# A third buffer for raw weights, and layer norms centred on ACT and scaled on GpSimd, in a hybrid decoder kernel on Trainium2

## The chip, the cores and the metric

The kernel runs on one core of a Trainium2 chip. Its engines run side by side, each through its own instructions in order: TensorE (PE in the profile; PEld its weight loads) multiplies matrices, VectorE (DVE) and ScalarE (ACT) do elementwise work, GpSimd (POOL) elementwise work of a slower kind, and SyncE (SP) issues the transfers. The metric is the device time of one execution in microseconds (us).

## The reference

Two layers over 512 tokens of width 1024, all in fp32. The four attention groups A to D are of 256 columns each; their inside is left out here.

```python
for l in range(DEPTH):                                  # DEPTH = 2
    h = x @ w_in[l]
    ...                                                 # out_a, out_b, out_c, out_d from parts of h
    mix = jnp.concatenate([out_a, out_b, out_c, out_d], axis=-1)
    y = _group_rmsnorm(mix, mix_g[l]) @ w_o[l]
    x = _layernorm(ALPHA * x + y, ln1_g[l], ln1_b[l])
    f = (jax.nn.silu(x @ w_gate[l]) * (x @ w_up[l])) @ w_down[l]      # width 2816
    x = _layernorm(ALPHA * x + f, ln2_g[l], ln2_b[l])

def _layernorm(x, g, b, eps=1e-5):
    mu = jnp.mean(x, axis=-1, keepdims=True)
    var = jnp.mean(jnp.square(x - mu), axis=-1, keepdims=True)
    return (x - mu) * lax.rsqrt(var + eps) * g + b
```

## The kernel before

The residual stream `x_res` stays on chip as four token tiles of 128 tokens by 1024, and is handled in halves of 512 columns. For matmuls x is also kept transposed (`xT`). To keep fp32 accuracy every operand is split into a high part (a rounded copy, on ACT or POOL) and a low part (operand minus high part, line 442, on DVE or POOL), and each product is made in three passes: high by high, high by low, low by high.

**Weights.** A `Chunk` is 128 x 1024 of weights: it is loaded into a raw buffer (`w_raw`, a ring of two), then `copy` makes the high part and `split_lo` the low part, into rings of their own (`w_hi`, `w_lo`; for the first two feature tiles `qk`, a ring that the attention has left by then). A loader takes the chunks in order as raw buffers come free, and a splitter follows.

**The order of the work** comes from a list scheduler in the program: every instruction is an `Op` with an engine, a cost and a priority, and the scheduler lays them one by one on the five in-order queues by their modelled earliest start and, within a slack, by priority. `sched.best` picks between engines the one that would end first. So an edit that changes one cost or engine moves others too.

**The stage around the change.** The last piece of a layer's attention is the out-projection of groups A and B, `out_proj(GA, GB)`. TensorE makes, per token tile and half, a product for A and one for B (six matmuls `ps<-w_hi/w_lo/v,mix` each, line 464), first for token tiles 0 and 1, then for 2 and 3. DVE adds each to `x_res` (line 1743); the add of B also sums the row for the norm. Then `layernorm` works tile by tile: ACT squares (L803), small DVE operations on columns of `lnst` (L810 to L840, L477 to L481, all 128 x 1), and two passes over each half on DVE:

```python
DVE.scalar_tensor_tensor(out=centred[c], in0=centred[c], scalar=st[:, 5:6], in1=gb[c], op0=ALU.add, op1=ALU.mult)   # L853: (x - mu) * gain
DVE.scalar_tensor_tensor(out=x[:, t, csl], in0=centred[c], scalar=st[:, 9:10], in1=bb[c], op0=ALU.mult, op1=ALU.add)  # L858: * rsqrt(var) + bias
```

The normed half is transposed by TensorE (L751, four 128 x 128), copied by ACT (the high part of xT, L453) and subtracted on DVE (its low part, L442); for ln1 another ACT copy (`keep`, L1801, a lower priority) stores the transposed tile for later. A tile counts as transposed for the next stage once that copy is laid on its queue. Next come the first two feature tiles, `up(0, 1)`: gate and up weights of 128 columns each, on half of the tokens at a time (24 matmuls `ps<-xT,qk` of 256 columns per weight and half). The first half of the tokens needs token tiles 0 and 1 only, and so can run while tiles 2 and 3 are still being normed.

ln1 stands at this place in both layers. ln2 of layer 0 follows the feed-forward (add on line 2003, gain in `mixf`, bias in `vd`), and the next layer's input projection uses `xT` behind it. ln2 of layer 1 ends the program; it is called with `hurry=True`. POOL also multiplies the residual by ALPHA after ln2 (L772).

Of the kernel before, what the change touches and what calls it, by code (L numbers as in the profile page):

```python
# [29 lines left out]
P = 128  # L30
S = 512
D = 1024
NT = S // P
# [13 lines left out]
GA, GB, GC, GD = range(4)  # L47
# [18 lines left out]
E_PE, E_ACT, E_DVE, E_POOL, E_SP = range(5)  # L66
# [22 lines left out]
def c_act(n, psum=True, extra=0):  # L89
    return (52.0 if psum else 94.0) + 0.832 * n + 93.0 * extra  # L90
# [14 lines left out]
def c_pool2(n):  # L105
    return 147.0 + 2.11 * n
# [13 lines left out]
class Sched:  # L120
# [232 lines left out]
def trunk(ctx: ExitStack, tc: tile.TileContext, d):  # L353
# [4 lines left out]
    spawn = sched.spawn  # L358
# [133 lines left out]
    class Chunk:  # L492


        def __init__(self, kt, n, parts, custom=None, rings=None, both=None, low=E_POOL, n_split=None, gate=None):
            self.kt, self.n, self.parts, self.custom = kt, n, parts, custom
            self.r_hi, self.r_lo = rings or (r_hi, r_lo)
            self.both, self.n_split, self.low, self.gate = both, n_split or n, low, gate
            self.raw = self.part = self.dep = self.loaded = None

        weight = 1

        def raw_room(self):
            return r_raw.ready()

        def view(self, tile_, n):
            return tile_[:, :self.kt * n].rearrange("p (k n) -> p k n", n=n)

        def load(self):
            self.raw = r_raw.take()  # L510
            e = NOW
            for k0, k1, c0, c1, src in self.parts:
                size = (k1 - k0) * (c1 - c0) * (2 if c1 - c0 < P else 1)
                e = yield from dma(self.view(self.raw.tile, self.n)[:, k0:k1, c0:c1], src, 1.46 * size / 1024, self.raw.dep)
            self.loaded = e
# [276 lines left out]
    def layernorm(t, vecs, st, dep, later, then, hurry=False):  # L792

        gb, bb, loaded, _ = vecs
        prio = LOW if hurry and t < NT - 1 else 0

        def square(c, dep):
            yield lambda: r_temp.ready()  # L800
            junk = r_temp.take()
            a = yield Op(E_ACT, c_act(512, False, 2), join(dep, junk.dep))
            ACT.activation(out=junk.tile, in_=x[:, t, c * 512:(c + 1) * 512], func=AF.Square, bias=st[:, 2:3], scale=1.0 / 32,  # L803
                           accum_out=st[:, 3 + c:4 + c])
            junk.give(a)
            squared[c] = a

        squared = {}
        e = yield Op(E_DVE, 130.0, dep)
        DVE.tensor_scalar(out=st[:, 2:3], in0=st[:, 0:1], scalar1=-1.0 / (32 * 512), scalar2=0.0, op0=ALU.mult, op1=ALU.add)  # L810
        spawn(square(0, e), 0, t - NT)
        second = yield later
        spawn(square(1, join(e, second)), 0, t - NT)
        e = yield Op(E_DVE, 130.0, second, prio)
        DVE.tensor_scalar(out=st[:, 5:6], in0=st[:, 1:2], scalar1=st[:, 0:1], scalar2=-1.0 / D, op0=ALU.add, op1=ALU.mult)
        centred = [x[:, t, :512], x[:, t, 512:]]
        held, early = [], {}
        if hurry and t == NT - 1:

            def centre(e):  # L820
                yield lambda: r_temp.ready(2)
                held.extend([r_temp.take(), r_temp.take()])
                for c in range(2):
                    g = yield Op(E_DVE, 663.0, join(e, loaded, held[c].dep))
                    DVE.scalar_tensor_tensor(out=held[c].tile, in0=centred[c], scalar=st[:, 5:6], in1=gb[c],
                                             op0=ALU.add, op1=ALU.mult)
                    centred[c] = held[c].tile
                early["done"] = g

            spawn(centre(e), 0, t - NT)  # L830
        b = yield Op(E_DVE, 130.0, second)
        DVE.tensor_scalar(out=st[:, 6:7], in0=st[:, 1:2], scalar1=st[:, 0:1], scalar2=1.0 / D, op0=ALU.subtract, op1=ALU.mult)
        a = yield lambda: squared.get(0)
        b = yield Op(E_DVE, 130.0, join(a, b))
        DVE.tensor_scalar(out=st[:, 7:8], in0=st[:, 6:7], scalar1=st[:, 6:7], scalar2=st[:, 3:4], op0=ALU.mult, op1=ALU.subtract)
        a = yield lambda: squared.get(1)

        def scale():
            r = yield Op(E_DVE, 130.0, join(a, b))
            DVE.tensor_scalar(out=st[:, 8:9], in0=st[:, 4:5], scalar1=st[:, 7:8], scalar2=1e-5, op0=ALU.subtract, op1=ALU.add)  # L840
            if hurry:
                squared["r"] = yield Op(E_POOL, 464.0, r)
                rsqrt(st[:, 9:10], st[:, 8:9])
            else:
                squared["r"] = yield from rsqrt_1(st[:, 9:10], st[:, 8:9], st[:, 10:13], r)

        spawn(scale(), 0, t - NT)
        if hurry and t == NT - 1:
            e = yield lambda: early.get("done")
        else:  # L850
            for c in range(2):
                e = yield Op(E_DVE, 663.0, join(a, e, loaded), prio)
                DVE.scalar_tensor_tensor(out=centred[c], in0=centred[c], scalar=st[:, 5:6], in1=gb[c], op0=ALU.add, op1=ALU.mult)  # L853
        r = yield lambda: squared.get("r")
        for c in range(2):
            csl = slice(c * 512, (c + 1) * 512)
            e = yield Op(E_DVE, 663.0, join(a, r, e), prio)
            DVE.scalar_tensor_tensor(out=x[:, t, csl], in0=centred[c], scalar=st[:, 9:10], in1=bb[c], op0=ALU.mult, op1=ALU.add)  # L858
            if c:
                x_dep[t] = e  # L860
            then(t, c, e)
        for h in held:
            h.give(e)


    def layer(l):
# [5 lines left out]
        at = {}  # L872
# [635 lines left out]
        class Uses:  # L1508


            def __init__(self, held, n):
                self.held, self.joint = held, Joint(n, held.give)
# [209 lines left out]
            return out  # L1722


        added = {(t, c): Joint(3) for t in range(NT) for c in range(2)}

        def out_proj(*groups, last=None):

            cs = {g: [Chunk(1, D, [(0, 1, 0, D, rows(d["w_o"][l], 2 * g + k, 1))],
                            both=r_v if len(groups) > 1 and g == groups[0] and k == 0 else None) for k in range(2)]  # L1730
                  for g in groups}
            chunks.extend(c for pair in cs.values() for c in pair)
            blocks = ((0, 1), (2, 3)) if len(groups) > 1 else ((0, 1, 2, 3),)
# [135 lines left out]
        def up(*js):  # L1869
            cs = {}  # L1870
            for j in js:
                for n in ("w_gate", "w_up"):
                    cs[n, j] = Chunk(KT, P, [(0, KT, 0, P, rows(d[n][l][:, j * P:(j + 1) * P], 0, KT))],
                                     rings=(r_qk, r_qk) if len(js) > 1 else None, low=E_DVE if len(js) > 1 else None,
                                     gate=(lambda: ("mix", GB) in at) if len(js) > 1 else None)
            chunks.extend(cs.values())
            toks = HALVES if len(js) > 1 else (ALL,)

            def unit():
                ps, ready = {}, {}  # L1880
# [250 lines left out]
        low = E_DVE  # L2131
# [140 lines left out]
```

## Time and profile before

| | |
|---|---|
| median of 3 runs | 1220.42 us (1219.75 to 1221.94) |
| the profiled execution | 1220.06 us, its span 1218.3 us |
| mean granted TensorE clock | 0.992 |
| instructions | 20162 |
| busy: PE, DVE, ACT, POOL | 97%, 73%, 56%, 20% of the span |
| ln1 of layer 0, about | 235 to 266 us |
| ln2 of layer 0, about | 592 to 617 us |
| ln1 of layer 1, about | 840 to 871 us |

A row of the timeline reads: start, duration, engine, line, operation, written tile <- read tiles, shape, how many instructions the row holds; in brackets the engine's idle time ahead of it and what ended that. A duration includes the tail of an instruction that already overlaps with the next on the same engine, so the distance of two starts is often shorter.

### The profile page before, as it was taken

Reading aid. Unit: us, or ns where it says so; the run is one execution under the profiler, and the core shown is the slowest. Engines: PE = TensorE matmul, PEld = TensorE weight load, DVE = VectorE, ACT = ScalarE, POOL = GpSimd, SP = SyncE. Lnnn points to the kernel's source line nnn. Section 1 sums busy time; section 2 is a strip of 40 time slices with the busy share of each in tenths; the row PEclk is TensorE's granted clock in tenths of the full one; section 3 lists DMA queues with packets and bytes.
Section 4 is the critical chain, followed back from the end, with each engine's and each line's share of the span. In section 5 each row is a group of like instructions: output and inputs, shape, how many; then the busy total and the mean of one; then the engine's idle time right before and its main releaser. Section 6 shows DMA issues by size and latency. Waiting matters only on the chain.

```text
span 1218.3 us, 20162 instructions
## 1 busy us (share of the span) xinstructions
PE 1180.2 (97%) x7589; PEld 1069.5 (88%) x7589; DVE 892.1 (73%) x1699; ACT 685.7 (56%) x1441; POOL 241.4 (20%) x243
## 2 busy tenths in 40 slices
PE   8999999989999999999999999999899999999996
PEld 7979878779999989998799797778899989899985
DVE  5669668799896649873655895788998947499626
ACT  4759869456564325553356797684665634256421
POOL 3552765300000000000034536543000000000001
PEclk9999999999999999999999999999999999999999
DMA  6312230423333133324233211203233341343341
GB/s 201 88 47 63 57 104 12 128 87 87 105 105 120 48 128 105 105 92 130 72 71 87 57 53 56 87 27 113 87 90 119 96 131 51 108 119 88 104 138 70
DMA packets 112162, 110.75 MB, mean 91 GB/s; under 512 B 9792, under 2 KB 94656, under 8 KB 112064
## 3 DMA queue, kind: packets, MB, share of 16 engines
q1 hardware_dynamic: 112064, 109.45, 29.9%
q8 instruction: 60, 0.98, 0.3%
q14 instruction: 38, 0.31, 0.1%
HBM read 107.34 MB, written 2.10 MB: 90 GB/s over the span
## 4 chain that ended last, share of the span: by engine, by line
PE 79%; DVE 9%; ACT 5%; issue 3%; POOL 2%; DMA 0%; POOLq 0%; SPq 0%; DVEq 0%; ACTq 0%
PE ps L464 76%; PE ps L1557 1%; DVE x_res L1743 1%; POOL w_lo L442 1%; PE ps L751 1%; DVE xT L442 1%; DVE qk L442 1%; ACT temp L1445 1%; DVE pt L442 1%; ACT pt L1363 1%; DVE x_res L858 1%; ACT xT L722 0%; DVE qk L444 0%; DVE temp L1306 0%; DVE augk L1092 0%
## 5 line engine op out<-in xcount | busy, mean ns | idle before, releaser
L464 PE MATMUL ps<-xT,w_hi 128*128 128x256 f32 (+1 forms) x1128 | 215.5, 318 | 0.0
L464 PEld LDWEIGHTS ps<-xT,w_hi 128*128 128x128 f32 x1128 | 162.4, 191 | 11.4
L464 PE MATMUL ps<-w_hi,qk 128*128 128x512 f32 (+1 forms) x560 | 171.5, 388 | 0.0
L464 PE MATMUL ps<-xT,w_lo 128*128 128x256 f32 (+1 forms) x888 | 166.0, 304 | 0.0
L722 ACT CAST w_hi<-w_raw 128x1024 fp32r<-128x1024 f32 (+2 forms) x91 | 92.8, 1021 | 108.1 <-PE ps L464 90.5
L442 POOL TENSOR_TENSOR w_lo<-w_raw,w_hi 128x1024 fp32r<-128x1024 f32 (+4 forms) x66 | 120.9, 1837 | 106.4 <-ACT w_hi L722 76.3
L442 DVE TENSOR_TENSOR w_lo<-w_raw,w_hi 128x1024 fp32r<-128x1024 f32 x47 | 57.6, 1225 | 111.6 <-ACT w_hi L722 111.5
L464 PEld LDWEIGHTS ps<-xT,w_lo 128*128 128x128 f32 x888 | 123.7, 191 | 7.3
L464 PEld LDWEIGHTS ps<-w_hi,qk 128*128 128x128 f32 x560 | 104.6, 189 | 20.9
L464 PE MATMUL ps<-w_hi,mix 128*128 128x512 f32 x352 | 110.1, 394 | 3.1 <-DVE xT L442 1.8
L464 PE MATMUL ps<-w_lo,qk 128*128 128x512 f32 (+1 forms) x280 | 108.2, 387 | 0.0
L1911 ACT COPY temp<-ps 128x256 f32<-128x256 f32 x120 | 44.7, 373 | 85.2 <-PE ps L464 84.7
L659 ACT CAST w_hi<-temp 128x512 fp32r<-128x512 f32 x78 | 48.3, 620 | 64.9 <-DVE temp L602 35.6
L772 POOL TENSOR_SCALAR x_res<-x_res 128x1024 f32<-128x1024 f32 x8 | 9.4, 1180 | 375.3 <-DVE lnst L840 357.2
L464 PEld LDWEIGHTS ps<-w_hi,mix 128*128 128x128 f32 x352 | 64.6, 188 | 16.4 <-issue 2.1
L442 DVE TENSOR_TENSOR w_hi<-temp,w_hi 128x512 fp32r<-128x512 f32 x78 | 53.2, 687 | 30.7 <-ACT w_hi L659 30.5
L467 POOL TENSOR_TENSOR lnst<-lnst,mhalf 128x1 f32<-128x1 f32 x4 | 3.9, 985 | 362.2 <-DVE lnst L840 362.2
L659 ACT CAST w_lo<-temp 128x512 fp32r<-128x512 f32 x82 | 50.8, 621 | 42.7 <-DVE temp L602 28.1
L464 PE MATMUL ps<-xT,qk 128*128 128x256 f32 x528 | 69.1, 291 | 2.0 <-DVE qk L442 2.0
L464 PE MATMUL ps<-w_lo,mix 128*128 128x512 f32 x176 | 69.0, 392 | 1.9 <-POOL w_lo L442 1.9
L464 PE MATMUL ps<-w_hi,xT 128*128 128x388 f32 (+1 forms) x256 | 69.1, 351 | 0.4 <-DVE qk L444 0.4
L464 PEld LDWEIGHTS ps<-xT,qk 128*128 128x128 f32 x528 | 66.8, 199 | 2.8 <-DVE qk L442 2.6
(234 smaller groups left out, 2692.5 us busy)
## 6 DMA issues: line engine op xcount, KB each, us to landing
w_raw<-in_w_down SPq DMA_DIRECT2D x44, 512.0 KB, 3.8
w_raw<-in_w_in SPq DMA_DIRECT2D x26, 512.0 KB, 3.7
w_raw<-in_w_gate SPq DMA_DIRECT2D x24, 512.0 KB, 3.7
w_raw<-in_w_up SPq DMA_DIRECT2D x24, 512.0 KB, 3.7
w_raw<-in_w_o SPq DMA_DIRECT2D x16, 512.0 KB, 3.7
vd<-in_w_up SPq DMA_DIRECT2D x10, 512.0 KB, 3.7
mixf<-in_w_up SPq DMA_DIRECT2D x10, 512.0 KB, 3.7
vd<-in_w_gate SPq DMA_DIRECT2D x10, 512.0 KB, 4.9
```

Of the source, the lines that this page charges most:

```text
L442: eng.tensor_tensor(out=lo, in0=src, in1=f(hi), op=ALU.subtract)
L464: PE.matmul(out, lhsT=lhsT, rhs=rhs, start=start, stop=stop, skip_group_check=True)
L659: ACT.copy(out=self.part[0], in_=src)
L722: ACT.copy(out=out, in_=in_ if psum is None else psum)
L751: PE.transpose(out=u.tile[:, k * P:(k + 1) * P], in_=x[:, t, kk * P:(kk + 1) * P], identity=ident)
L772: POOL.tensor_scalar(out=x[:, t], in0=x[:, t], scalar1=ALPHA, scalar2=0.0, op0=ALU.mult, op1=ALU.add)
L858: DVE.scalar_tensor_tensor(out=x[:, t, csl], in0=centred[c], scalar=st[:, 9:10], in1=bb[c], op0=ALU.mult, op1=ALU.add)
L1363: ACT.copy(out=dst[0], in_=src)
L1445: ACT.activation(out=p[:, s_], in_=ps.tile[:, s_], func=AF.Exp, bias=r[:, nm + j:nm + j + 1], scale=1.0 if scale is None else scale[:, i:i ...
L1557: PE.transpose(out=u.tile[:, k * P:(k + 1) * P], in_=p.tile[:, k * P:(k + 1) * P], identity=ident)
L1743: DVE.scalar_tensor_tensor(out=x[:, t, csl], in0=ps.tile, scalar=rs[:, t:t + 1], in1=x[:, t, csl], op0=ALU.mult, op1=ALU.add, accum_out=st ...
L1911: ACT.copy(out=dst, in_=src)
```

## The change

Three edits.

1. A third raw buffer: once group D is done with its tile, the `vd` buffer may hold raw weights for the chunks of `out_proj(GA, GB)` and `up(0, 1)` (`more=vd_free`).
2. For the first feature tiles' low parts the engine is no longer fixed to DVE but chosen by `sched.best` between DVE and POOL (`low=None`).
3. In the norms without `hurry` (ln1 of both layers, ln2 of layer 0) the pass of L853 becomes two: ACT adds the negative mean in place (`Identity` with a bias, new L827), and POOL multiplies by the gain in place (new L829). The last pass (now L876) stays on DVE. Per token tile and half one DVE operation goes, one ACT and one POOL operation come; 24 of each over the program.

```diff
+        def raw_rings(self):
+            return (r_raw, r_vd) if self.more and self.more() else (r_raw,)
+
         def raw_room(self):
-            return r_raw.ready()
+            free = [x for r in self.raw_rings() for x in r.free if x is not None]
+            return min(free, key=max) if free else None
...
         def load(self):
-            self.raw = r_raw.take()
+            ring = min((r for r in self.raw_rings() if r.ready() is not None), key=lambda r: max(r.ready()))
+            self.raw = ring.take([P, 1024], F32)
...
+        def centre(c, e):
+
+            e = yield Op(E_ACT, c_act(512, False, 1), e)
+            ACT.activation(out=centred[c], in_=centred[c], func=AF.Identity, bias=st[:, 5:6])
+            middle[c] = yield Op(E_POOL, c_pool2(512), join(e, loaded))
+            POOL.tensor_tensor(out=centred[c], in0=centred[c], in1=gb[c], op=ALU.mult)
...
             for c in range(2):
-                e = yield Op(E_DVE, 663.0, join(a, e, loaded), prio)
-                DVE.scalar_tensor_tensor(out=centred[c], in0=centred[c], scalar=st[:, 5:6], in1=gb[c], op0=ALU.add, op1=ALU.mult)
+                if hurry:
+                    e = yield Op(E_DVE, 663.0, join(a, e, loaded), prio)
+                    DVE.scalar_tensor_tensor(out=centred[c], in0=centred[c], scalar=st[:, 5:6], in1=gb[c], op0=ALU.add, op1=ALU.mult)
+                else:
+                    spawn(centre(c, join(a, e)), 0, t - NT)
         r = yield lambda: squared.get("r")
         for c in range(2):
             csl = slice(c * 512, (c + 1) * 512)
+            if not hurry:
+                e = yield lambda: middle.get(c)
...
+        def vd_free():
+            return ("mix", GD) in at
+
...
-                            both=r_v if len(groups) > 1 and g == groups[0] and k == 0 else None) for k in range(2)]
+                            both=r_v if len(groups) > 1 and g == groups[0] and k == 0 else None,
+                            more=vd_free if len(groups) > 1 else None) for k in range(2)]
...
-                                     rings=(r_qk, r_qk) if len(js) > 1 else None, low=E_DVE if len(js) > 1 else None,
-                                     gate=(lambda: ("mix", GB) in at) if len(js) > 1 else None)
+                                     rings=(r_qk, r_qk) if len(js) > 1 else None, low=None,
+                                     gate=(lambda: ("mix", GB) in at) if len(js) > 1 else None,
+                                     more=vd_free if len(js) > 1 else None)
```

New lines shift the numbers: L751 becomes L756, L858 becomes L876, L1743 becomes L1765, L1801 becomes L1823, the others of the norm by 5 to 23. What the scheduler then lays on the queues shows at three places, all at the end of layer 0's out-projection (layer 1 has the same pattern).

TensorE, before: the product of group B for token tile 3 (two halves, `ps6` and `ps0`) and what follows. The first feature matmul stands right behind it, with 23 more of its kind; the transposes of token tile 2 come after these.

```order
L464 MATMUL ps6_2838<-w_lo1_2653,mix1_2615 128x512
L464 MATMUL ps0_2848<-w_hi0_2613,mix1_2615 128x512 x2
L464 MATMUL ps0_2848<-w_lo0_2614,mix1_2615 128x512
L464 MATMUL ps0_2848<-w_hi1_2652,mix1_2615 128x512 x2
L464 MATMUL ps0_2848<-w_lo1_2653,mix1_2615 128x512
L464 MATMUL ps4_2872<-xT_2683,qk0_2681 128x256 x2
L464 MATMUL ps4_2872<-xT_2683,qk8_2682 128x256
```

TensorE, after: the same product (`ps6`, `ps5`) and what follows.

```order
L464 MATMUL ps6_2830<-w_lo1_2655,mix1_2617 128x512
L464 MATMUL ps5_2850<-w_hi0_2615,mix1_2617 128x512 x2
L464 MATMUL ps5_2850<-w_lo0_2616,mix1_2617 128x512
L464 MATMUL ps5_2850<-w_hi1_2654,mix1_2617 128x512 x2
L464 MATMUL ps5_2850<-w_lo1_2655,mix1_2617 128x512
L756 MATMUL ps1_2901<-ident_72,x_res_73 128x128 x4
L756 MATMUL ps4_2905<-ident_72,x_res_73 128x128 x4
L464 MATMUL ps3_2868<-xT_2685,qk0_2683 128x256 x2
```

The transposes of token tile 2 (L756) now stand ahead of the first feature half.

DVE, before: the end of token tile 2's norm (`lnst_2790`) among the adds for token tile 3 (L1743; `ps6_2838` and `ps0_2848` are the two halves of B's product above). `qk2` is the low part of the first up weight.

```order
L1743 SCALAR_TENSOR_TENSOR x_res_73,lnst_2821<-ps6_2838,rsg_2660,x_res_73 128x512
L479 TENSOR_SCALAR lnst_2790<-lnst_2790 128x1
L810 TENSOR_SCALAR lnst_2821<-lnst_2821 128x1
L481 TENSOR_SCALAR lnst_2790<-lnst_2790 128x1
L1743 SCALAR_TENSOR_TENSOR x_res_73<-ps5_2769,rsg_2414,x_res_73 128x512
L858 SCALAR_TENSOR_TENSOR x_res_73<-x_res_73,lnst_2790,lnv2_2621 128x512
L1743 SCALAR_TENSOR_TENSOR x_res_73,lnst_2821<-ps0_2848,rsg_2660,x_res_73 128x512
L858 SCALAR_TENSOR_TENSOR x_res_73<-x_res_73,lnst_2790,lnv3_2622 128x512
L815 TENSOR_SCALAR lnst_2821<-lnst_2821 128x1
L832 TENSOR_SCALAR lnst_2821<-lnst_2821 128x1
L442 TENSOR_TENSOR qk2_2708<-w_raw0_2680,qk4_2707 128x1024
```

DVE, after: token tile 2's statistics are `lnst_2793`, token tile 3's `lnst_2829`; `ps5_2850` is the second half of B's product.

```order
L1765 SCALAR_TENSOR_TENSOR x_res_73,lnst_2829<-ps5_2850,rsg_2662,x_res_73 128x512
L442 TENSOR_TENSOR xT_2685<-ps2_2832,xT_2685 128x4x128
L820 TENSOR_SCALAR lnst_2829<-lnst_2829 128x1
L845 TENSOR_SCALAR lnst_2829<-lnst_2829 128x1
L442 TENSOR_TENSOR qk2_2691<-w_raw0_2653,qk4_2690 128x1024
L477 TENSOR_SCALAR lnst_2793<-lnst_2793 128x1
L848 TENSOR_SCALAR lnst_2829<-lnst_2829 128x1
L479 TENSOR_SCALAR lnst_2793<-lnst_2793 128x1
L853 TENSOR_SCALAR lnst_2829<-lnst_2829 128x1
L481 TENSOR_SCALAR lnst_2793<-lnst_2793 128x1
L876 SCALAR_TENSOR_TENSOR x_res_73<-x_res_73,lnst_2793,lnv2_2623 128x512
L876 SCALAR_TENSOR_TENSOR x_res_73<-x_res_73,lnst_2793,lnv3_2624 128x512
```

Both final passes of token tile 2 (L876) now stand behind the add of token tile 3's second half and behind the low part `qk2`; before, the first stood ahead of that add and both ahead of `qk2`.

POOL, before, around the power that belongs to a group's RMS norm (L467); `w_lo1` is the last low part of w_o, `qk7` the high part of the second gate weight, L772 the scaling of the residual in ln2.

```order
L442 TENSOR_TENSOR w_lo0_2614<-w_raw1_2488,w_hi0_2613 128x1024
L467 TENSOR_TENSOR rsg_2660<-rsg_2660,mhalf_76 128x4
L442 TENSOR_TENSOR w_lo1_2653<-w_raw0_2559,w_hi1_2652 128x1024
L724 TENSOR_SCALAR qk7_2926<-w_raw1_2706 128x1024
L772 TENSOR_SCALAR x_res_73<-x_res_73 128x1024 x3
L442 TENSOR_TENSOR w_lo0_6720<-w_raw0_6699,w_hi0_6719 128x1024
```

POOL, after, from the same power on; `lnv0` and `lnv1` are the gain's two halves in ln1, `mixf0` the gain in ln2.

```order
L467 TENSOR_TENSOR rsg_2662<-rsg_2662,mhalf_76 128x4
L442 TENSOR_TENSOR w_lo1_2655<-vd0_2492,w_hi1_2654 128x1024
L829 TENSOR_TENSOR x_res_73<-x_res_73,lnv0_2613 128x512
L829 TENSOR_TENSOR x_res_73<-x_res_73,lnv1_2614 128x512
L829 TENSOR_TENSOR x_res_73<-x_res_73,lnv0_2613 128x512
L829 TENSOR_TENSOR x_res_73<-x_res_73,lnv1_2614 128x512
L829 TENSOR_TENSOR x_res_73<-x_res_73,lnv0_2613 128x512
L829 TENSOR_TENSOR x_res_73<-x_res_73,lnv1_2614 128x512
L729 TENSOR_SCALAR qk7_2887<-vd0_2682 128x1024
L829 TENSOR_TENSOR x_res_73<-x_res_73,lnv0_2613 128x512
L829 TENSOR_TENSOR x_res_73<-x_res_73,lnv1_2614 128x512
```

Eight products (L829) now stand in POOL's queue behind `w_lo1`, the copy of a feature weight (L729) among them.

More of the change, by code (lines that the diff above doesn't have):

```diff
@@ L492, in trunk, with __init__ @@
     class Chunk:
-        def __init__(self, kt, n, parts, custom=None, rings=None, both=None, low=E_POOL, n_split=None, gate=None):
+        def __init__(self, kt, n, parts, custom=None, rings=None, both=None, low=E_POOL, n_split=None, gate=None, more=None):
             self.kt, self.n, self.parts, self.custom = kt, n, parts, custom
             self.r_hi, self.r_lo = rings or (r_hi, r_lo)
-            self.both, self.n_split, self.low, self.gate = both, n_split or n, low, gate
+            self.both, self.n_split, self.low, self.gate, self.more = both, n_split or n, low, gate, more
             self.raw = self.part = self.dep = self.loaded = None
         weight = 1
+        def raw_rings(self):
+            return (r_raw, r_vd) if self.more and self.more() else (r_raw,)
         def raw_room(self):
-            return r_raw.ready()
+            free = [x for r in self.raw_rings() for x in r.free if x is not None]
+            return min(free, key=max) if free else None
         def view(self, tile_, n):
@@ L816, in layernorm @@
         centred = [x[:, t, :512], x[:, t, 512:]]
-        held, early = [], {}
+        held, early, middle = [], {}, {}
+        def centre(c, e):
[3 more added lines that the diff above has]
+            POOL.tensor_tensor(out=centred[c], in0=centred[c], in1=gb[c], op=ALU.mult)
         if hurry and t == NT - 1:
```

## The prediction

> **What bounds the kernel now.** I read the page's busy shares and its chain first, then the chain's stretches around the norms in the timeline of TensorE, and last the rows of the engines that release it there.
>
> ```profile
> PE 1180.2 (97%) x7589; PEld 1069.5 (88%) x7589; DVE 892.1 (73%) x1699; ACT 685.7 (56%) x1441; POOL 241.4 (20%) x243
> ...
> PE 79%; DVE 9%; ACT 5%; issue 3%; POOL 2%; DMA 0%; POOLq 0%; SPq 0%; DVEq 0%; ACTq 0%
> ```
>
> TensorE is busy 97% of the span and is 79% of the chain. The edits leave its matmuls as they are, so they can only change how long it stands idle, and only in the three places where the changed norms run: the end of the out-projection of layers 0 and 1 (ln1) and the end of layer 0's feed-forward (ln2). TensorE's rows with a wait, layer 0's ln1 first:
>
> ```profile
> 234.44 0.50 PE L464 MATMUL ps<-w_lo,mix 128*128 128x512 f32 x1 [1.42 <-POOL w_lo L442]
> ...
> 249.82 0.73 PE L464 MATMUL ps<-w_hi,mix 128*128 128x512 f32 x2 [0.66 <-DVE x_res L1743]
> ...
> 252.68 3.03 PE L464 MATMUL ps<-xT,qk 128*128 128x256 f32 x24
> 257.00 0.63 PE L751 MATMUL ps<-ident,x_res 128*128 128x128 f32 x4 [1.29 <-DVE x_res L858]
> 258.33 0.63 PE L751 MATMUL ps<-ident,x_res 128*128 128x128 f32 x4 [0.70 <-DVE x_res L858]
> ...
> 259.62 3.13 PE L464 MATMUL ps<-xT,qk 128*128 128x256 f32 x24 [0.43 <-DVE qk L442]
> 263.94 0.74 PE L464 MATMUL ps<-xT,qk 128*128 128x256 f32 x4 [1.19 <-DVE qk L442]
> ...
> 266.17 6.00 PE L464 MATMUL ps<-xT,qk 128*128 128x256 f32 x48
> ```
>
> The brackets give the idle time before a row and who ended it. L464 on `w_lo,mix` is the out-projection, L751 transposes a normed token tile, `xT,qk` are the first feature tiles. The waits are 1.42 for the last low part of w_o, 0.66 at token tile 3, 1.29 and 0.70 for token tile 2's norm, 0.43 and 1.19 for low parts of the feature weights: 5.69 us. The 0.66 is for a PSUM bank that an add (L1743) had to free. Layer 1:
>
> ```profile
> 839.20 0.50 PE L464 MATMUL ps<-w_lo,mix 128*128 128x512 f32 x1 [0.51 <-POOL w_lo L442]
> ...
> 854.59 0.73 PE L464 MATMUL ps<-w_hi,mix 128*128 128x512 f32 x2 [0.66 <-DVE x_res L1743]
> ...
> 861.76 0.63 PE L751 MATMUL ps<-ident,x_res 128*128 128x128 f32 x4 [1.28 <-DVE x_res L858]
> 863.10 0.63 PE L751 MATMUL ps<-ident,x_res 128*128 128x128 f32 x4 [0.71 <-DVE x_res L858]
> ...
> 864.38 5.12 PE L464 MATMUL ps<-xT,qk 128*128 128x256 f32 x28 [0.43 <-DVE qk L442]
> ```
>
> Here they are 0.51, 0.66, 1.28, 0.71 and 0.43. The last row's 28 matmuls take 5.12, against 3.03 for the 24 of layer 0's 252.68 row (0.126 each): another 1.59 of small stalls, the place of layer 0's 1.19. In ln2:
>
> ```profile
> 608.02 0.71 PE L751 MATMUL ps<-ident,x_res 128*128 128x128 f32 x4 [2.15 <-DVE x_res L858]
> 608.96 1.09 PE L751 MATMUL ps<-ident,x_res 128*128 128x128 f32 x4 [0.23 <-DVE lnst L840]
> 609.70 4.82 PE L464 MATMUL ps<-xT,qk 128*128 128x256 f32 x30
> ```
>
> 2.15 + 0.23, and 30 matmuls in 4.82 where 30 × 0.126 is 3.78: 1.04 of small stalls. What all the edits together could win is therefore 5.69 + 5.18 + 3.42 = 14.3 us, and no more. The engine that ends most of these waits is full:
>
> ```profile
> 231.00:266.20 35.20, 29.51 (x169) 24.57 (x167) 32.27 (x80) 17.62 (x40) 4.42 (x3) 1.00 0.23 65
> ```
>
> In these 35.2 us DVE works 32.27 (92%), ACT 17.62, POOL 4.42. Moving work off DVE is aimed at the right engine; the question is what path the moved work takes.
>
> **The change part by part.** Prices, all of one profiled execution:
>
> ```profile
> 256.77 0.74 DVE L1743 SCALAR_TENSOR_TENSOR x_res<-ps,rsg,x_res 128x512 f32<-128x512 f32 x1
> ...
> 257.44 0.74 DVE L858 SCALAR_TENSOR_TENSOR x_res<-x_res,lnst,lnv 128x512 f32<-128x512 f32 x1
> 258.11 0.20 DVE L815 TENSOR_SCALAR lnst<-lnst 128x1 f32<-128x1 f32 x1
> 258.23 0.20 DVE L832 TENSOR_SCALAR lnst<-lnst 128x1 f32<-128x1 f32 x1
> 258.35 1.21 DVE L442 TENSOR_TENSOR qk<-w_raw,qk 128x1024 fp32r<-128x1024 f32 x1
> 259.49 0.26 DVE L835 TENSOR_SCALAR lnst<-lnst 128x1 f32<-128x1 f32 x1
> ...
> 261.30 0.68 DVE L442 TENSOR_TENSOR xT<-ps,xT 128x512 fp32r<-128x512 f32 x1
> 261.90 0.14 DVE L479 TENSOR_SCALAR lnst<-lnst 128x1 f32<-128x1 f32 x1
> ...
> 236.97 0.72 ACT L803 ACTIVATE temp<-x_res,lnst 128x512 f32<-128x512 f32 x1 [2.64 <-DVE lnst L810]
> ...
> 225.17 1.29 POOL L732 TENSOR_TENSOR temp<-temp,temp 128x512 f32<-128x512 f32 x1 [5.66 <-issue]
> ...
> 232.02 2.37 POOL L442 TENSOR_TENSOR w_lo<-w_raw,w_hi 128x1024 fp32r<-128x1024 f32 x1
> ```
>
> Starts one behind the other give pitches: a 512-wide DVE operation 0.67, a small one 0.12, a low part of 1024 1.14, an xT low part 0.60, and from DVE's end (257.44 + 0.74) to TensorE (258.33) 0.15. The new ACT centring has ACT's L803 square of the same shape as nearest row, 0.72; the POOL multiply has POOL's own 128x512 product, 1.29. Neither operation stood on these engines before. The POOL one lies between POOL's smallest row below (1.02) and its 1024-wide difference (2.37); I take the row of equal width. ACT's price enters no term below, since the floor worked out there is DVE's.
>
> *Norm.* Per token tile two DVE operations go (2 × 0.67 = 1.34); two ACT operations (1.4) and two on POOL (2.6) come, in series: the first half is ready 0.72 + 1.29 after the squares instead of 0.74, later by 1.3, the second by about 1.9, and POOL needs 2.6 per tile. Over three norms DVE loses 24 × 0.67 = 16 us of work, POOL gains 24 × 1.29 = 31. DVE's own share matters only where TensorE waits for it.
>
> What the longer path meets is in-order queues. In ln1 ACT's centring pushes ACT's copies of the transposed tiles back; the feature tiles are only issued behind these, so on TensorE token tile 2's transposes now stand ahead of the first 24 feature matmuls (3.03 us of cover gone). On DVE, token tile 2's final operation (L876) stands behind the add of token tile 3's second half, which needs the out-projection's last matmul. So from that matmul on, TensorE has nothing until DVE has done the add 0.67, an xT low part 0.60, two small ones 0.24, a feature low part 1.14, five small ones 0.60 and L876 0.74, with two hand-offs of 0.15: 4.3, and the second half 0.67 later while the first half's transposes fill 0.35: 4.6 in all. That is a floor by the order of the rows, however fast POOL is. Before, the same place cost 1.29 + 0.70; but the low parts' waits behind it go, since both low parts are done by then (0.43 + 1.19 in layer 0, 0.43 + 1.59 in layer 1), and so does the bank's 0.66, since the other group's adds for tile 3 now come earlier on DVE. Without any further delay: layer 0 4.6 − 4.27 = +0.3, layer 1 4.6 − 4.67 = −0.1.
>
> *What POOL and DVE do to each other.*
>
> ```profile
> 226.28 0.75 DVE L444 SCALAR_TENSOR_TENSOR mix<-mixf,mg,mix 128x512 fp32r<-128x512 f32 x1
> ...
> 227.85 2.37 DVE L444 SCALAR_TENSOR_TENSOR mix<-mixf,mg,mix 128x512 fp32r<-128x512 f32 x1
> ...
> 227.27 2.40 POOL L442 TENSOR_TENSOR w_lo<-w_raw,w_hi 128x1024 fp32r<-128x1024 f32 x1 [0.81 <-ACT w_hi L722]
> ```
>
> The same DVE operation takes 0.75 alone and 2.37 when POOL's 2.40 row is under way: it starts at 227.85 and ends at 230.22, 0.55 after POOL does. It stood still. The other direction:
>
> ```profile
> 231.02 1.02 POOL L467 TENSOR_TENSOR rsg<-rsg,mhalf 128x4 f32<-128x4 f32 x1 [1.36 <-DVE rsg L1502]
> ...
> 231.92 0.75 DVE L1743 SCALAR_TENSOR_TENSOR x_res<-ps,rsg,x_res 128x512 f32<-128x512 f32 x1 [0.32 <-PE ps L464]
> ...
> 832.95 2.40 POOL L442 TENSOR_TENSOR w_lo<-w_raw,w_hi 128x1024 fp32r<-128x1024 f32 x1 [2.46 <-ACT w_hi L722]
> 835.31 1.48 POOL L467 TENSOR_TENSOR rsg<-rsg,mhalf 128x4 f32<-128x4 f32 x1
> ...
> 833.52 2.38 DVE L444 SCALAR_TENSOR_TENSOR mix<-mixf,mg,mix 128x512 fp32r<-128x512 f32 x1
> ```
>
> In layer 1 the stalled DVE row ends at 835.90; POOL's next one, 1.02 alone, takes 1.48, so the one that had waited went first and POOL paid. L444 takes two operands from SBUF, as do L876 and the low parts of weights; an add has one operand in PSUM, and the one of 231.92 took its usual 0.75 beside POOL's row of 232.02. Now POOL has eight multiplies among eight L876 in each ln1. Following the rows: L876 of token tile 0 comes due while POOL multiplies tile 1; each half waits for one product, and its second half's transposes are late by 0 to 1.3; I take 1.0. At tile 2 the feature low part waits for the second product and L876's second half for POOL's copy of a feature weight, 0 to 2 × 1.29 = 2.6; I take 0.7, near the low end, since ACT releases tile 2's products early enough that most of them is over.
>
> [...]
>
> *Third raw buffer.* It lets raw weights of w_o and the first feature tiles land earlier; four of SP's transfers move ahead, one of them past the loads of ln1's gain and bias, which are not due for several us. TensorE's waits of 1.42 and 0.51 do not go with it: the low part they wait for is queued on POOL behind a power (L467) that waits for DVE's stalled L444, not behind a transfer. [...]
>
> *Low parts to GpSimd.* The choice is by earliest end; in the built order all of the four stay on DVE. 0.
>
> *ln2.* No feature half stands before tile 2's transposes here either, so no cover is lost.
>
> ```profile
> 607.22 0.75 DVE L858 SCALAR_TENSOR_TENSOR x_res<-x_res,lnst,vd 128x512 f32<-128x512 f32 x1
> ...
> 608.07 0.74 DVE L858 SCALAR_TENSOR_TENSOR x_res<-x_res,lnst,vd 128x512 f32<-128x512 f32 x1
> ```
>
> DVE's L858 starts at 607.22 and 608.07; two products fewer ahead let the first start about 0.2 earlier, POOL's scaling of the residual (in its queue now mixed with the multiplies) can hold the second by up to 0.8, a row of 1.29 that began 0.5 earlier. Of the 1.04 in small stalls most comes from late low parts and should go. −0.2 + 0.4 − 0.7 = −0.5, between −1.2 and +0.8.
>
> **Sum.** Layer 0: 0.85 + 1.0 + 4.6 + 0.7 − 4.27 = +2.9 (from +0.3 to +5.4). Layer 1: 1.0 + 4.6 + 0.7 − 4.67 = +1.6 (−0.1 to +3.8). ln2 −0.5 (−1.2 to +0.8). Together +4.0, from −1.0 to +10.0. The profiled execution took 1220.06 (span 1218.3, 1.8 around it), 0.4 below the median of 1220.42, so 1220.06 + 4.0 = 1224.
>
> **The rivals.**
> - *The meetings are missed, no change.* POOL's products fall between DVE's; the floor of 4.6 then about equals what was there. For it: DVE's smalls and adds, most of its rows, do not stall. Against: eight L876 in about 16 us with 10 us of POOL work between them. −1.0 to +2.4: 1219 to 1222.5, middle 1221.
> - *DVE relieved, faster.* The mechanism is 16 us less on an engine at 92%. It decides if ln2's 2.15 + 0.23 go as well as the small stalls (−3.4) and both ln1 stay at their floor: 1220.06 − 3.4 + 0.2 = 1216.9; with the w_lo waits gone too (1.42 + 0.51), 1215.0. I take 1216.5. Against it, L858 in ln2 follows the add of tile 3, not the removed products. [...]
> - *POOL becomes the bound.* Eight products of 1.29 plus the copy fill 11.4 us of each ln1; if each of L876 doubles, the high ends hold: +6 to +10, about 1228.
>
> **How the numbers follow.** A measurement here tells 0.2%, 2.4 us, from no change. Forecast (+2.4 to +6, 1222.9 to 1226): 0.44. POOL as the bound: 0.09. Missed meetings: 0.28. Faster: 0.19. So slower 0.53, same 0.28, faster 0.19. The range reaches from 1216.5, the middle of the faster case, to 1228, the middle of the worst; some 0.15 is left out. The forecast's own range is 1222.9 to 1226.
>
> **What would show it.** Right: TensorE's L756 row for token tile 2 in each ln1 shows a wait of some 4 to 5 us after L876, with the 24 feature matmuls behind it and their low-part waits gone; some L876 rows at 1.3 to 2 us beside POOL L829; layer 0's wait for w_lo near 2.3. Wrong: L876 all at 0.74, L829 far from 1.29, or ACT's L827 well over 0.72. What would upset the sum most is a shorter queue in front of token tile 2's L876 than the order says.

## The result, and the profile after

The changed kernel takes 1228.33 us (median of 6 runs, 1226.63 to 1230.97) against 1220.72 before: 7.6 us more, a ratio of 1.0062 [1.005, 1.0073]. The profiled execution has a span of 1226.9, 8.6 above that of before. The page's busy line of the changed kernel, and its chain:

```profile
PE 1183.7 (96%) x7589; PEld 1072.6 (87%) x7589; DVE 889.7 (73%) x1675; ACT 699.8 (57%) x1465; POOL 279.0 (23%) x267
...
PE 79%; DVE 10%; ACT 5%; issue 3%; POOL 2%; DMA 1%; SPq 0%; POOLq 0%; DVEq 0%; ACTq 0%
```

The 8.6 us fall into two parts. TensorE is busy 3.5 us longer (1183.7 against 1180.2) for the same 7589 matmuls: they run slower. The other 5.1 us are idle time.

Where they arise shows when the starts of like matmuls in the two profiled executions are compared. Layer 0's ln1 takes 4.0 us longer (1.6 of idle time, 2.4 of slower matmuls), layer 1's 3.65 (2.8 and 0.8), ln2 0.45 less. Stages that no edit touches (at 8, 76 and 758 us) add 1.7 net, nearly all of it matmuls at another clock, and behind the last matmul the end is 0.3 shorter.

In layer 0's ln1 TensorE's timeline reads:

```profile
235.15 0.50 PE L464 MATMUL ps<-w_lo,mix 128*128 128x512 f32 x1 [1.99 <-POOL w_lo L442]
...
236.32 1.05 PE L464 MATMUL ps<-w_hi,mix 128*128 128x512 f32 x2
...
259.19 1.11 PE L756 MATMUL ps<-ident,x_res 128*128 128x128 f32 x4 [4.85 <-DVE x_res L876]
260.72 1.09 PE L756 MATMUL ps<-ident,x_res 128*128 128x128 f32 x4 [0.42 <-DVE x_res L876]
261.46 4.64 PE L464 MATMUL ps<-xT,qk 128*128 128x256 f32 x30
```

The wait before token tile 2's transposes is 4.85 + 0.42 = 5.27. But look at the durations too: two `w_hi,mix` matmuls take 1.05 where their like took 0.62, four transposes 1.1 where they took 0.63. The view by stretches says why. A row gives a stretch and its length, the busy time and instructions of PE, PEld, DVE, ACT and POOL, and last the granted TensorE clock, the DMA share and GB/s:

```profile
237.00:239.00 2.00, 2.00 (x6) 1.51 (x6) 1.09 (x4) 0.85 (x3) 0.00 (x0) 0.50 1.12 337
261.00:263.00 2.00, 2.00 (x11) 2.00 (x10) 2.00 (x3) 1.00 (x2) 2.00 (x2) 0.50 0.00 0
870.00:872.00 2.00, 2.00 (x11) 2.00 (x11) 2.00 (x5) 0.62 (x2) 2.00 (x2) 0.50 0.00 0
```

TensorE runs at half its clock behind these waits. The clock records of the trace show such stretches as 3.41 or 6.83 us long; below, a *half-speed window* is one of 3.41 us at a clock of 0.50, that is, up to 1.7 us lost. Layer 1 looks the same:

```profile
867.55 1.11 PE L756 MATMUL ps<-ident,x_res 128*128 128x128 f32 x4 [4.82 <-DVE x_res L876]
869.09 1.09 PE L756 MATMUL ps<-ident,x_res 128*128 128x128 f32 x4 [0.42 <-DVE x_res L876]
869.83 5.80 PE L464 MATMUL ps<-xT,qk 128*128 128x256 f32 x30
```

ln2 of the changed kernel waits a little more than before and sees no slow clock (1.00 from 606 to 622 us):

```profile
612.01 0.66 PE L756 MATMUL ps<-ident,x_res 128*128 128x128 f32 x4 [1.97 <-DVE x_res L876]
613.54 0.63 PE L756 MATMUL ps<-ident,x_res 128*128 128x128 f32 x4 [0.88 <-DVE lnst L845]
613.92 5.99 PE L464 MATMUL ps<-xT,qk 128*128 128x256 f32 x48
```

DVE's rows and POOL's of the same stretch of layer 0 (x2 is both halves of a tile):

```profile
244.81 2.45 DVE L876 SCALAR_TENSOR_TENSOR x_res<-x_res,lnst,lnv 128x512 f32<-128x512 f32 x2
...
256.25 1.21 DVE L442 TENSOR_TENSOR qk<-w_raw,qk 128x1024 fp32r<-128x1024 f32 x1
...
258.37 2.20 DVE L876 SCALAR_TENSOR_TENSOR x_res<-x_res,lnst,lnv 128x512 f32<-128x512 f32 x2
```

```profile
255.00 3.58 POOL L829 TENSOR_TENSOR x_res<-x_res,lnv 128x512 f32<-128x512 f32 x2 [8.28 <-ACT x_res L827]
...
258.56 1.48 POOL L729 TENSOR_SCALAR qk<-vd 128x1024 fp32r<-128x1024 f32 x1
```

Two L876 alone take 0.67 + 0.74 = 1.4; here 2.45 and 2.20, so single halves stood still by 0.8 to 1.0. At token tile 2 DVE's low part came first (1.21, undisturbed) and it was POOL's pair of products that waited (3.58; its first pair, at 240.14, took 2.56).

### The profile page after: what moved, and what is told of

It is laid out like the page before. It is cut to its first block, busy times and chain, and to the rows that moved or that the text cites. A ratio compares the mean times of both kernels' runs of the same rounds, so it can differ in the third digit from the quotient of the medians.

```text
span 1226.9 us, 20190 instructions
## 1 busy us (share of the span) xinstructions
PE 1183.7 (96%) x7589; PEld 1072.6 (87%) x7589; DVE 889.7 (73%) x1675; ACT 699.8 (57%) x1465; POOL 279.0 (23%) x267
## 4 chain that ended last, share of the span: by engine, by line
PE 79%; DVE 10%; ACT 5%; issue 3%; POOL 2%; DMA 1%; SPq 0%; POOLq 0%; DVEq 0%; ACTq 0%
PE ps L464 76%; PE ps L1575 1%; DVE x_res L876 1%; DVE qk L442 1%; DVE x_res L1765 1%; ACT temp L1463 1%; POOL w_lo L442 1%; PE ps L756 1%; ACT pt L1381 1%; DVE pt L442 1%; DVE xT L442 1%; DMA x_res<-in_x 1%; ACT xT L727 0%; DVE qk L444 0%; DVE temp L1324 0%
## 5 line engine op out<-in xcount | busy, mean ns | idle before, releaser
L442 POOL TENSOR_TENSOR w_lo<-w_raw,w_hi 128x1024 fp32r<-128x1024 f32 (+4 forms) x64 | 116.0, 1819 | 99.8 <-ACT w_hi L727 75.6
L829 POOL TENSOR_TENSOR x_res<-x_res,mixf 128x512 f32<-128x512 f32 x8 | 11.6, 1471 | 339.4 <-ACT x_res L827 339.4
L467 POOL TENSOR_TENSOR lnst<-lnst,mhalf 128x1 f32<-128x1 f32 x4 | 3.9, 986 | 345.3 <-DVE lnst L853 345.3
```

The lines of the kernel that those rows point to most:

```text
L442: eng.tensor_tensor(out=lo, in0=src, in1=f(hi), op=ALU.subtract)
L829: POOL.tensor_tensor(out=centred[c], in0=centred[c], in1=gb[c], op=ALU.mult)
```

## The experiments

The theory from this trace: (1) the time is lost because the 24 feature matmuls no longer cover token tile 2's norm, and (2) the clock makes each longer wait cost more than itself. The rivals: the norm's longer path over ACT and POOL with the stalls between POOL and DVE, the third buffer, or idle time alone. The ratios are to the kernel before, timed beside each run (medians 1220.48 to 1220.73). A ratio is not the quotient of the two medians, and where they differ (`nocover`: 1.0054 by medians) the text goes by the interval too.

| run | median us | ratio, 95% interval |
|---|---|---|
| changed kernel | 1228.33 | 1.0062 [1.005, 1.0073] |
| cover | 1221.02 | 1.0001 [0.9992, 1.001] |
| warm | 1225.35 | 1.0037 [1.0025, 1.0049] |
| norms | 1221.37 | 0.9999 [0.999, 1.0009] |
| third | 1229.08 | 1.0066 [1.0049, 1.0083] |
| third_dve | 1224.62 | 1.003 [1.002, 1.004] |
| nocover | 1227.03 | 1.0039 [1.0025, 1.0052] |
| fill | 1218.31 | 0.998 [0.9971, 0.9989] |
| cover_fill | 1218.11 | 0.9969 [0.9957, 0.9981] |
| late_low | 1227.08 | 1.0047 [1.0031, 1.0063] |
| late_low_fill | 1220.85 | 0.9999 [0.9989, 1.0009] |
| norms_fill | 1217.06 | 0.9973 [0.9961, 0.9985] |

**cover.** In the changed kernel, a tile counts as transposed without waiting for `keep`:

```diff
             if keep:
-                e3 = yield from keep(h, tok, u.tile.rearrange("p (k n) -> p k n", k=4), e)
-                u.give(join(e2, e3))
+                def store():
+                    e3 = yield from keep(h, tok, u.tile.rearrange("p (k n) -> p k n", k=4), e)
+                    u.give(join(e2, e3))
+                spawn(store(), 1)
```

> The changed kernel with one edit: ACT's copy of a transposed tile (L1823) no longer counts towards the tile being ready, so the first 24 feature matmuls are laid ahead of token tile 2's transposes again. Theory (lost cover plus slow clock): the wait of 4.85 falls by about the 3.0 of these matmuls, to 1.5 to 2.2, in both ln1; at that length the clock stays full or dips for half as long; 1228.3 - 2 x 2.5 - 1 to 3 = 1220.5 to 1223. [...]

Measured 1221.02: as the theory had it, the whole loss is gone with ACT, POOL, DVE and the buffer edit all in place. Counted between like matmuls, each ln1 is 1.3 shorter than in the kernel before; the feature matmuls behind (0.75 per layer, with a wait of 0.49 for a low part that was not there before) and ln2 (0.6) give most of it back. TensorE at layer 0's tile 2:

```profile
261.01 0.66 PE L756 MATMUL ps<-ident,x_res 128*128 128x128 f32 x4 [1.13 <-DVE x_res L878]
262.45 0.66 PE L756 MATMUL ps<-ident,x_res 128*128 128x128 f32 x4 [0.43 <-DVE x_res L878]
```

1.13 instead of 4.85, and no half-speed stretch there (0.66, not 1.11).

**warm.** In the changed kernel, ahead of token tile 2's first transposes in ln1:

```diff
+            for k in range(36 if keep and t == 2 and h == 0 else 0):
+                PE.transpose(out=u.tile[:, k % 4 * P:(k % 4 + 1) * P], in_=x[:, 0, k % 8 * P:(k % 8 + 1) * P], identity=ident)
```

> The changed kernel with 36 more transposes of token tile 0 on TensorE in front of token tile 2's first transposes in both ln1; their results are overwritten by the real ones. They fill about 4 of the 4.85 us that TensorE waits, and move nothing else. Theory: the granted clock stays at 1.00 behind the wait, and the half-speed stretches of 259 to 265 and 867 to 875 go: 1.5 to 2 us less per layer, 1224 to 1225.5. Rival (the slow clock only goes with the wait and costs nothing, or comes from something else): 1228 or a little more.

Measured 1225.35, 3.0 less, although TensorE has 72 more instructions and the wait for L876 ends no earlier (24.0 us behind the row that waits for `w_lo`, in both kernels):

```profile
253.80 4.09 PE L755 MATMUL ps<-ident,x_res 128*128 128x128 f32 x36
258.82 0.66 PE L758 MATMUL ps<-ident,x_res 128*128 128x128 f32 x4 [0.92 <-DVE x_res L878]
```

```profile
261.00:263.00 2.00, 2.00 (x19) 2.00 (x19) 2.00 (x3) 0.59 (x1) 2.00 (x2) 1.00 0.00 0
```

In the same two microseconds as above the clock is 1.00, and 19 matmuls fit where 11 did. So the slow clock is a cost of its own, but the 3.0 are not its price. Between like matmuls of the two profiled executions the filling gains 0.6 in layer 0's ln1 and 0.8 in layer 1's, where one half-speed window stays (at 866.87) against the expectation; the rest lies in stages that the edit does not touch. Filling also costs: the second wait grows from 0.42 to 0.88.

**norms** and **third**: each edit alone. `norms` is the changed kernel with `more=None` and `low=E_DVE` as before; `third` the kernel before with the first two edits only.

> Only the norm edit: raw weights keep two buffers and the low parts stay fixed on DVE. In the order that follows, 20 of the 24 first feature matmuls stand ahead of token tile 2's transposes. Theory: most of the cover is kept, so the wait there is about 2.5, with little slow clock: 1220.5 to 1224. Rival (the norm's longer path is the cost whatever stands around it): 1226 to 1229.

> Only the third raw buffer and the free choice of engine for the low parts; the norms as before. Theory: the wait for the last low part of w_o in layer 0 is 1.99 again instead of 1.42, with the half-speed stretch behind it (about 1.6 us), the waits for feature low parts (0.43 + 1.19) go: 1219 to 1222. Rival (the earlier low part is harmless): 1218 to 1220.

`norms` at 1221.37 can't be told from before. It keeps its cover, better than expected: 27 feature matmuls stand ahead of tile 2's transposes, which then don't wait at all; what waits is the first feature half, by 1.33. The rival that the longer path costs by itself falls. Nor is the edit without effect: between like matmuls `norms` gains 1.6 and 1.5 in the two ln1 over the kernel before, and loses 1.3 behind each, where the feature matmuls wait 0.95 for a low part from DVE.

```profile
254.47 0.28 PE L464 MATMUL ps<-xT,qk 128*128 128x256 f32 x1
256.07 3.36 PE L464 MATMUL ps<-xT,qk 128*128 128x256 f32 x26 [1.33 <-DVE xT L442]
259.52 1.38 PE L756 MATMUL ps<-ident,x_res 128*128 128x128 f32 x8
```

`third` at 1229.08 was a miss for both sides. In the order that followed, the free choice sent the second gate and up weights' low parts to POOL, and DVE stood still beside them. POOL's rows and DVE's in layer 1:

```profile
851.54 2.70 POOL L442 TENSOR_TENSOR qk<-vd,qk 128x1024 fp32r<-128x1024 f32 x1
...
855.78 2.86 POOL L442 TENSOR_TENSOR qk<-w_raw,qk 128x1024 fp32r<-128x1024 f32 x1
```

```profile
852.10 2.69 DVE L858 SCALAR_TENSOR_TENSOR x_res<-x_res,lnst,lnv 128x512 f32<-128x512 f32 x1
...
856.48 2.71 DVE L863 SCALAR_TENSOR_TENSOR x_res<-x_res,lnst,lnv 128x512 f32<-128x512 f32 x1
```

**third_dve.** The same, `low=E_DVE if len(js) > 1 else None` kept:

> Only the third raw buffer; low parts fixed on DVE, norms as before. In the run with the free choice, two low parts went to POOL and DVE's norm rows stood still beside them at 2.7 us. Theory (that choice was the cost there, the buffer is nearly harmless): w_lo's wait 1.99 instead of 1.42 in layer 0, and at most one half-speed window (1.7) behind it: 1219.5 to 1222.5. Rival (the buffer itself costs, by the order that it sets): 1226 or more.

Measured 1224.62: some 4.5 of `third` were the choice of engine. That figure is rough, since three executions of `third` took about 1227 and three about 1231.5. The buffer alone still costs 3.9 us, more than expected. Its idle time in the profiled execution (1221.5 − 1183.9 = 37.6) is that of before (1218.3 − 1180.2 = 38.1); what is new is `w_lo`'s wait

```profile
234.75 0.50 PE L464 MATMUL ps<-w_lo,mix 128*128 128x512 f32 x1 [2.00 <-POOL w_lo L442]
```

and two more half-speed windows than before (235 to 240, 259 to 264), both in layer 0's ln1. Between like matmuls that ln1 is 2.0 longer (3.1 of slower matmuls, 1.1 less idle), and the feature matmuls behind each ln1 are 0.75 longer, with a wait of 0.49 for a low part. This is the account of one execution, 1.4 below the median. The two slowest (1226.83 and 1227.35) have granted clocks of 0.990 and 0.991, no lower than its 0.989, so what makes them slow stays open.

**nocover.** The kernel before with one line changed in `up`:

```diff
-                            xr = yield lambda: x_ready(tok)
+                            xr = yield lambda: x_ready(tok) if len(js) == 1 or xT_at[2] is not None else None
```

> The kernel before with nothing moved but the 24 first feature matmuls of each ln1, now laid behind token tile 2's transposes. Theory: the waits at those transposes become 1.29 + 3.03 + 0.70 = 5.0, the waits for feature low parts behind them (0.43, 1.19; 0.43) go, and one more half-speed window of 3.4 us (1.7 lost) comes per layer: idle + 1.4 and + 2.6, clock + 1.7 to + 3.4, in all + 5.7 to + 7.4: 1226 to 1228. Rival (idle time alone counts, the clock costs nothing): 1223.5 to 1225. Second rival (the lost cover matters only with the norm's longer path): 1220 to 1222.

Measured 1227.03, in the theory's range. The second rival falls. The interval of the ratio (3.0 to 6.3 us) alone does not exclude the first, idle time without the clock; the trace does: of the 5.3 by which the two ln1 grow between like matmuls (2.6 and 2.7), idle time makes 2.8 and slower matmuls 2.5, with two half-speed windows at each of the two waits. The lost cover alone, without any edit of the change, gives most of the change's loss (4.0 and 3.65 in the same places of the changed kernel):

```profile
258.89 1.08 PE L751 MATMUL ps<-ident,x_res 128*128 128x128 f32 x4 [4.17 <-DVE x_res L858]
260.22 1.09 PE L751 MATMUL ps<-ident,x_res 128*128 128x128 f32 x4 [0.25 <-DVE x_res L858]
260.96 5.23 PE L464 MATMUL ps<-xT,qk 128*128 128x256 f32 x28
```

```profile
257.00:261.00 4.00, 1.86 (x9) 1.52 (x9) 4.00 (x13) 2.10 (x5) 0.00 (x0) 0.60 0.00 0
261.00:265.00 4.00, 4.00 (x22) 4.00 (x21) 4.00 (x11) 2.02 (x5) 0.00 (x0) 0.54 0.45 131
```

**fill** and **cover_fill.** The kernel before, and the one of `cover`, with transposes of the identity ahead of the waits that the expectation lists:

```diff
+            for k in range((0 if t != 2 else (8, 4)[h] if keep else 14 if not h and after_ln else 0)):
+                PE.transpose(out=u.tile[:, k % 4 * P:(k % 4 + 1) * P], in_=ident, identity=ident)
...
+        for k in range({0: 8, 3: 8, 7: 14, 8: 4}.get(calls["sums"], 0)):
+            PE.transpose(out=u.tile[:, k % 4 * P:(k % 4 + 1) * P], in_=ident, identity=ident)
```

> The kernel before with useless transposes of the identity on TensorE in front of eight waits: 8, 8, 14 and 4 ahead of four row sums that wait for POOL (at 75, 204, 752 and 808 us), 14 ahead of token tile 2's transposes in ln2, 8 and 4 ahead of its two transposes in both ln1. Results are overwritten. Theory: the three half-speed windows of before (608, 755, 864) go, 1.7 each, some waits being met late by 0.2: 1215 to 1218. Rival (the windows come from the amount of work, or cost nothing): 1220 to 1222.

> The kernel of the run with the cover put back, with the same useless transposes as in the filled kernel before. Theory: its half-speed windows (206 to 213, 612, 759, some 6.8 us lost of 1221) go down to one or two: 1215.5 to 1219. Rival: 1221.

1218.31 (0.3 above its range) and 1218.11: 2.4 and 2.9 below their own unfilled kernels. That is what filling wins net; it isn't the price of the windows. Of the three windows named, all are gone in the trace of `fill`, but between like matmuls only the stage of the one at 755 got shorter (1.6); ln2 is 0.4 longer and layer 1's ln1 the same, as there the filling cost what it saved. A new window stands at 182, in another stage. The kernel before also has a fourth window, at 7.75, where nothing was filled.

**late_low.** The kernel of `cover`, the first feature weights split later, and on DVE (`low=E_DVE` again, a line not shown here):

```diff
-                                     gate=(lambda: ("mix", GB) in at) if len(js) > 1 else None,
+                                     gate=(lambda: "bt" in at) if len(js) > 1 else None,
...
                 if st is not None:
+                    at["bt"] = e
                     done_[c] = e
```

> The changed kernel with the cover put back, and the first feature weights split only once the first add of group B is laid, their low parts on DVE: the first gate tile's low part no longer stands on DVE beside POOL's power. Theory: layer 0's wait for w_lo is 1.42 again, not 1.99, and the half-speed window that followed it in some runs goes: 1218.5 to 1220.5 against 1221.0 with the cover alone. Rival (that wait is not the low part's doing): 1221 and 1.99 still.

A miss: 1227.08. Its own term came out as expected, but the scheduler laid the rest differently:

```profile
233.48 0.50 PE L464 MATMUL ps<-w_lo,mix 128*128 128x512 f32 x1 [1.42 <-POOL w_lo L442]
245.05 0.66 PE L756 MATMUL ps<-ident,x_res 128*128 128x128 f32 x4 [1.02 <-DVE x_res L878]
252.74 3.26 PE L464 MATMUL ps<-xT,qk 128*128 128x256 f32 x25 [0.51 <-DVE xT L442]
```

1.42 again, so its growth to 1.99 was the early low part's doing; behind it stand 1.02, 0.51 and a wait of 2.30 at token tile 2, in both layers. The profiled execution, at 1223.33 the fastest of the six, has one half-speed window at each 2.30. Its granted clock is 0.992; the other five (1225.4 to 1228.1) have 0.988 to 0.990, which by an estimate from these figures is 2.4 to 4.9 us more of lost clock, about as much as they are longer.

**late_low_fill** and **norms_fill.** The last kernel filled, and the norm edit alone with the cover edit, filled.

> The same with the useless transposes in front of eight waits. Theory: 1215 to 1218, with at most one half-speed window in the middle of the span. Rival (filling and the late low part win the same windows, not two): 1218 as with the cover and the fill.

> The norm edit alone (no third buffer, low parts on DVE) with the cover edit and the useless transposes. Theory: 1221.4 for the norm edit alone, less two to three half-speed windows of 1.7: 1216 to 1218.5. Rival: no better than the filled kernel before, 1218.3, as the norm edit itself wins nothing.

`late_low_fill`, 1220.85, is 6.2 below `late_low` but far from its range. `norms_fill`, 1217.06, beats both kernels: 0.9973 [0.9961, 0.9985] to the one before. Its trace shows no half-speed window ahead of the last microseconds. Against `fill` (1218.31) it wins 1.2, which the intervals don't separate.

## Why the prediction was right or wrong

The sign was right, for the reason given first; the size, 4.0 against 7.6, was not, and the time lies just above the range. That it comes near the 1228 of the rival with POOL as the bound is chance: eight products did not fill ln1, and only some L876 rows doubled.

- *Token tile 2's wait.* Forecast 4.6 + 0.7 = 5.3 in each ln1; measured 5.27 and 5.24. The reading of the order was right, and `cover` and `nocover` show that this is the mechanism. That even the size fits is chance. The 0.7 stood for meetings with POOL. In the trace the first wait is 0.55 over the floor of 4.3 by DVE alone: its add starts 0.40 behind the last matmul, not 0.15, and the five small operations take 0.99, not 0.60. The bank's 0.66 and the waits for feature low parts went as said.
- *The step that failed: a wait was priced at its own length.* No term of the sum has the clock. In the changed kernel two half-speed windows go with each of the 4.8 us waits (in layer 0 they begin 2.7 us before its end), and one follows the wait for `w_lo`. Slower matmuls make up 3.2 us of the two ln1, 2.4 and 0.8, for which the sum has nothing; `warm` took 1.4 of the time there back by keeping TensorE busy.
- *The idle time was near, in part by chance.* By stage it came to +1.6, +2.8 and +0.8 (layer 0, layer 1, ln2) against terms of +2.9, +1.6 and −0.5. In layer 0 the 1.0 of token tile 0 did not arrive; in layer 1 the sum took off 1.59 that was never idle time, as the next point shows.
- *The misread rows.* The prediction took 1.59 us in layer 1 and 1.04 in ln2 for small stalls on late low parts. They were this same slow clock, in the kernel before. So the sum's credit for them in layer 1 was false: the one window there became two.

```profile
608.00:610.00 2.00, 1.75 (x9) 1.49 (x10) 2.00 (x5) 0.89 (x3) 0.00 (x0) 0.62 0.00 0
610.00:612.00 2.00, 2.00 (x12) 2.00 (x11) 2.00 (x6) 1.53 (x2) 1.63 (x1) 0.52 0.00 0
864.00:866.00 2.00, 1.61 (x8) 1.62 (x9) 2.00 (x6) 0.76 (x3) 0.00 (x0) 0.62 0.13 34
866.00:868.00 2.00, 2.00 (x11) 2.00 (x11) 2.00 (x6) 1.15 (x2) 0.00 (x0) 0.52 0.77 228
```

  A view by stretches of 2 us would have shown it then. The prediction's one stretch, 35 us of layer 0, read 1.00, as no window lies in it.
- *The first gate tile's low part.* The 0.85 in layer 0's sum stood for DVE's low part delaying `w_lo`, whose wait it put near 2.3; it was the author's estimate, and no run shows it. In the trace the low part runs on DVE from 231.67 at its usual 1.21, `w_lo` on POOL takes 2.93 against 2.37 in the kernel before, and the wait grows by 0.57, to 1.99. One half-speed window comes with it; the matmuls behind it took 1.5 us longer in all, more than the wait grew.
- *POOL against DVE.* The stalls came (L876 2.45 and 2.20 for a pair), but the 1.0 taken at token tile 0 did not reach TensorE in layer 0, where the slow clock had made it late itself; in layer 1 it was 0.69. At tile 2 the low part did not wait for POOL's second product, as the prediction took it to; there POOL paid. The second half of L876 did wait 0.8 for POOL's copy of a feature weight, but behind the half-speed transposes only 0.42 of idle time was left; in `warm`, with these at full clock in layer 0, it is 0.88.
- *ln2.* −0.5 forecast. By the start times of like matmuls TensorE gains 0.45 there, but not by the terms given: the waits grew by 0.8 (1.97 + 0.88 + 0.29 against 2.38), and what went is the half-speed window. The terms have no part in that: the same wait of 1.97 was followed by a window in three of the five traces that have it, and what decides is not shown.
- *Low parts to GpSimd, 0.* Right in this kernel; in `third` the same edit costs some 4.5.
- *Which edit.* The prediction charged the norm edit with nearly all. Alone it costs nothing; the third buffer alone costs 3.9. Neither alone loses the cover (in `norms` 27 and in `third_dve` 24 feature matmuls stand ahead of token tile 2's transposes); with both in it is lost.

What stays open: why a wait of 2.18 at 755 us is followed by one window in the kernel before (there 2.19) and by two in the changed one. The stage is one that no edit touches, and two windows stand there in 3 of the 13 traces; with one trace per kernel it isn't shown whether the change has a part in it. Also open is how much of the 7.6 between the medians is the two ln1 and how much is windows elsewhere.

## What to carry to other kernels

Price a wait of the main engine together with the clock behind it: look at the granted clock in stretches of a few microseconds before calling a slow group "stalls". Where work is reordered by a scheduler, look first for what used to cover a wait; two edits, neither of which removes that cover alone, can remove it together. And where a wait can't be removed, useless matmuls in it may pay: they took 2.4 us off the kernel before, though not at every wait.

## What the runs showed of the hardware

- In these traces the slow clock comes in whole windows: all 46 stretches in the 13 traces ahead of the last microseconds are 3.4 or 6.8 us long and lost 1.7 or 3.4 us, that is one or two windows of 3.4 us at half speed.
- Over these traces, all 4 waits above 4 us (4.16 to 4.85) went with two windows. Of 16 waits between 2.1 and 2.35 us 15 were followed by at least one. The wait for `w_lo` was followed by one in 5 of 6 traces where it was 1.98 to 2.00, and in none of 7 where it was 1.42 or 1.43. Nine traces have a wait of 1.2 at 73 to 76 us and one of 1.3 at 203 to 206 us; each was followed by one or two windows in four of them. The wait of 1.23 to 1.25 at 677 to 685 us, in all 13, was followed by none.
- Length alone does not decide: the 13 waits of 1.74 to 1.76 at 780 to 791 us were followed by none. Within a trace the stretches start whole multiples of 3.413 us apart: in the kernel before at 7.75, 608.50, 755.27 and 864.50 us, that is at distances of 176.0, 43.0 and 32.0 times 3.413. What decides whether a wait of some 2 us is followed by a window is not shown: in ln2 the wait of 2.15 in the kernel before was, the 1.97 in the changed kernel was not.
